# Group norm's inverse deviations on Pool, the rotation tables' memory given back earlier, and two sets of small products placed later

## The chip, the cores and the metric

One core of a Trainium2 chip runs the whole layer in one launch. The metric is device time in microseconds (us). Engines by their names in the profile: PE does the matmuls and PEld loads their weights, DVE is the vector engine, ACT the scalar engine, POOL (Pool in the text) the GpSimd engine, SP issues DMAs.

## The reference

One inference step of a hybrid decoder layer on 256 prompt positions and 8 sequences of 8 new positions, 320 columns in all. It is fp32 throughout. Cut to what matters here:

```
h = rms_norm(x, norm_mix);  u, q, k, v, g = split(h @ w_in)
# S5 group: 64 channel groups, diagonal complex state, scan over positions
xs = associative_scan(a, bu);  y = Re(C xs) + d*u;  y = gelu(y);  s5 = y * sigmoid(y @ w_glu + b_glu)
# retention group: 8 heads of 128, rotary q and k, decay mask
o = ((q k^T) * mask) v + (q r) * q_decay;   r_new = r * decay + (k * k_decay)^T v
mu, var = mean(o), mean((o - mu)^2)                       # group norm over the 128 of a head
o = (o - mu) * rsqrt(var + eps) * ret_gn_w;  ret = silu(g) * o
x = x + concat(s5, ret) @ w_out
x = x + (silu(h2 @ w_gate) * (h2 @ w_up)) @ w_ffn_out,  h2 = rms_norm(x, norm_ffn)
y = rms_norm(x, norm_final)
```

## The kernel before

All activations lie transposed: features on the 128 partitions, the 320 columns in the free dimension. Every large matmul takes a weight block of 128x128 as the stationary operand and 320 columns as the moving one. Each weight is split into a rounded part `hi` (ACT, L128) and a rest `lo` (DVE, L129), the activations likewise, and three matmuls (L139, L140, L141) make one k-step. Blocks of eight k-steps of weights are loaded by SP into three rotating buffers.

The first part of the program (to about 400 us) is the input projection. Between its k-steps stand the small products of eight retention heads and of eight S5 chunks. Where they stand is set by a planner that runs when the program is built: each head and each chunk is a generator, which issues some instructions and then yields a delay; a clock that counts issued matmuls decides after which k-step it goes on. The delays are in the table `DL`. PE and Pool execute their instructions in exactly the order in which the program issues them. DVE and ACT get an order from a scheduler that knows priorities and a model of durations. Every engine works its queue off in order: an instruction that waits holds all behind it.

Names for the steps below. A head `h`: `head_k` transposes the rotated keys `k_` into `pst` and makes the scores `pss`; DVE masks them into `sm` and `smp`. `head_v` transposes the values (`pst2`, which ACT scales into `vT`), makes the outputs `po` and the state product `psr`. Then comes the group norm: DVE's `bn_stats` and `bn_aggr` give mean and variance `mv`, a chain of small instructions on 128x4 makes `gy` (inverse deviation and shift), ACT makes the normalised `on` from `po` and `gy` (L694), and PE transposes it into `pn` (L105), from where it goes to `retp`.

A chunk `c`: DVE makes `bl` and `cl` from the parameters, PE transposes `bl` into `pt`, makes `pk_` (the short kernel) and `pb` (the inputs), DVE rotates by the tables `tab`, scans and rotates back into `xp`, and PE makes the outputs `py`.

`s5_params` makes the parameters on DVE, in scratch space that lies in the two `cl` buffers. Its last products are `lx0`. It then lets Pool clear both `cl` buffers (L448), which has to wait until DVE has read the scratch space for the last time. Pool also makes the rotation tables (`s5_tables`), in four groups of eight pairs.

After the projection: `fin` makes the final states with the last column of `tab`; `split_r` splits the heads' results into `r4a` (heads 0 to 3, in the buffer of the tag "tab") and `r4b`; then `w_out` with `r4a` first, the GLU, `w_out` with its output, and the FFN from about 533 us to the end. `ffn_norm` makes the norm of the FFN's input between the first k-steps of the FFN.

Of the kernel before, what the change touches and what calls it, by code (L numbers as in the profile page):

```python
# [12 lines left out]
F32 = mybir.dt.float32  # L13
# [3 lines left out]
ALU = mybir.AluOpType  # L17
ADD, SUB, MUL = ALU.add, ALU.subtract, ALU.mult
PSUM = bass.MemoryType.PSUM

P = 128
# [9 lines left out]
EPS = 1e-6  # L31
LPAST = 2048
CH = 4
NCP = NP // CH
NC = N // CH
TAIL = ((0, 1), (1, 2), (2, 3), (3, 5), (5, 8), (8, 11))
NPAIR = 32
# [7 lines left out]
def hybrid_kernel(ctx, tc, xT, w_in, w_out, w_glu, w_fi, w_fo, vecs, s5p, bc, x0,  # L45
# [3 lines left out]
    pe, act, dve, pool, sp = nc.tensor, nc.scalar, nc.vector, nc.gpsimd, nc.sync  # L49

    cst = ctx.enter_context(tc.tile_pool(name="cst", bufs=1))
# [8 lines left out]
    make_identity(nc, ident)  # L60
    ones = cst.tile([P, P], F32, name="ones")
    pool.memset(ones, 1.0)
    vec = cst.tile([P, vecs.shape[1]], F32, name="vec")
    bmk = cst.tile([P, 4], F32, name="bmk")

# [2 lines left out]
    o = 0  # L68
# [97 lines left out]
    def ts(out, a, s1, o1, s2=None, o2=None):  # L166
        if o2 is None:
            dve.tensor_scalar(out, a, s1, None, o1)
        else:
            dve.tensor_scalar(out, a, s1, s2, o1, o2)  # L170
        return out
# [5 lines left out]
    def stt(out, a, s, b, o1, o2):  # L177
        dve.scalar_tensor_tensor(out, a, s, b, o1, o2)
        return out

    def rsqrt(t, y, tmp):

        ts(y.bitcast(I32), t.bitcast(I32), -0.5, MUL, float(0x1EF759DF), ADD)
        for _ in range(3):
            tt(tmp, y, y, MUL)
            tt(tmp, tmp, t, MUL)
            stt(y, tmp, 1.5, y, ADD, MUL)
# [104 lines left out]
    prm = s5.tile([P, 3, NPAIR], F32, name="prm")  # L292
    x0t = s5.tile([P, 2, NPAIR, NB], F32, name="x0t")
    tab = s5.tile([P, 2, NPAIR, NCP], F32, name="tab", tag="tab", bufs=1)
    rr = s5.tile([P, NPAIR], F32, name="rr")
    r4 = s5.tile([P, NPAIR], F32, name="r4")
    ff = s5.tile([P, 2, NPAIR], F32, name="ff")
# [159 lines left out]
    def s5_tables(ec, es, g):  # L457
        js = slice(8 * g, 8 * g + 8)
        pool.memset(tab[:, 0, js, 0:1], 1.0)
        pool.memset(tab[:, 1, js, 0:1], 0.0)  # L460
        m, lev = 1, 2
        while m < NCP:
            shm = [P, 8, m]
            er = ec[:, lev, js].unsqueeze(2)
            ei = es[:, lev, js].unsqueeze(2)
            c0, s0 = tab[:, 0, js, 0:m], tab[:, 1, js, 0:m]
            c1, s1 = tab[:, 0, js, m:2 * m], tab[:, 1, js, m:2 * m]
            if m == 1:
                pool.tensor_copy(c1, er)
                pool.tensor_copy(s1, ei)  # L470
            else:
                er, ei = er.to_broadcast(shm), ei.to_broadcast(shm)
                ta = s5.tile([P, 8, 32], F32, name="ta", tag="ta", bufs=1)[:, :, :m]
                pool.tensor_tensor(c1, c0, er, MUL)
                pool.tensor_tensor(ta, s0, ei, MUL)
                pool.tensor_tensor(c1, c1, ta, SUB)
                pool.tensor_tensor(ta, s0, er, MUL)
                pool.tensor_tensor(s1, c0, ei, MUL)
                pool.tensor_tensor(s1, s1, ta, ADD)
            m *= 2  # L480
            lev += 1
            yield 2.0 if g else 0.0


# [10 lines left out]
    def s5_chunk(c):  # L495
# [21 lines left out]
        for w_, pc in ((0, gpc), (1, lpc)):  # L517
# [14 lines left out]
            for g in range(2):  # L532
                ps_, hs = slice(64 * g, 64 * g + 64), slice(16 * g, 16 * g + 16)
                if w_:
                    tt(cl[ps_, 0, :, 1:, hs], m1[ps_, 0:4], m2[ps_, 4:8], SUB)
                    tt(cl[ps_, 1, :, 1:, hs], m1[ps_, 4:8], m2[ps_, 0:4], SUB)
        yield DL["b1"]
        bst = s5.tile([P, 8, P], F32, name="bst", tag="bst", bufs=1)[:, 0:4]
        pt = misc("pt")
        for i in range(4):  # L540
# [94 lines left out]
        return a  # L635

    def head_k(h, q_, qg, k_, R):
        yield DL["k"]
        pst = misc("pst")
        for i, s in enumerate(STARTS):  # L640
            tr(pst[:, P * i:P * i + P], k_[:, s:s + P])
        kd = mp.tile([P, 2, P], F32, name="kd", tag="kd", bufs=1)
        for i in range(2):
            act.mul(kd[:, i], pst[:, P * i:P * i + P], kdc[:, h, i:i + 1])
        act.mul(kv[64:128, h], pst[64:128, 2 * P:3 * P], kdc[64:128, h, 2:3])
        pss = misc("pss")
        mm(0.43, pss[:, 0:256], k_[:, 0:P], q_[:, 0:256], start=True, stop=True)
        mm(0.22, pss[:, 256:384], k_[:, P:256], q_[:, P:256], start=True, stop=True)
        mm(0.22, pss[:, 384:448], k_[:, 192:320], q_[:, 256:320], start=True, stop=True)
        sm = mp.tile([P, 384], F32, name="sm", tag="sm", bufs=1)  # L650
        mk = R["mk"]
        tt(sm[:, 0:256], pss[:, 0:256], mk[:, 0:NP], MUL)
        tt(sm[:, 256:384], pss[:, 256:384], mk[:, 0:P], MUL)
        tt(smp[64:128, :, 0:NS], pss[64:128, 384:448].rearrange("p (b t) -> p b t", t=NS),
           mk[64:128, NP:320].rearrange("p (b t) -> p b t", t=NS), MUL)
        R["kd"], R["sm"] = kd, sm

    def head_v(h, v_, qg, rt, R):
        yield DL["v"]
        pst2 = misc("pst2")  # L660
        for i, s in enumerate(STARTS):
            tr(pst2[:, P * i:P * i + P], v_[:, s:s + P])
        vT = mp.tile([P, 3, P], F32, name="vT", tag="vT", bufs=1)
        for i in range(3):
            act.mul(vT[:, i], pst2[:, P * i:P * i + P], rtok[:, i:i + 1])
        act.copy(kv[0:64, h], vT[64:128, 2])
        yield DL["o"]
        kd, sm = R["kd"], R["sm"]

        po = ps_v.tile([P, 4, P], F32, name="po", tag="po", bufs=1)  # L670
        mm(0.22, po[:, 0], sm[:, 0:P], vT[:, 0], start=True, stop=True)
        mm(0.22, po[:, 1], sm[:, P:256], vT[:, 0], start=True, stop=False)
        mm(0.22, po[:, 1], sm[:, 256:384], vT[:, 1], start=False, stop=True)

        for g in range(2):
            mm(0.22, po[:, 2 + g], smp[:, 4 * g:4 * g + 4].rearrange("p b t -> p (b t)"), vT[:, 2],
               start=g == 0, stop=False, skip_group_check=True)
        for g in range(2):
            for j in range(4):
                mm(0.06, po[32 * j:32 * j + 32, 2 + g], qg[:, 4 * g + j], rt[:, 4 * g + j], start=False,  # L680
                   stop=True, tile_position=(0, 32 * j), skip_group_check=True)
        st = mp.tile([P, 4, 6], F32, name="st", tag="st", bufs=1)
        mv = mp.tile([P, 2, 4], F32, name="mv", tag="mv", bufs=1)
        y = mp.tile([P, 2, 4], F32, name="gy", tag="gy", bufs=1)
        with tc.high_priority(offset=GN):
            for i in range(4):
                dve.bn_stats(st[:, i], po[:, i])
                dve.bn_aggr(mv[:, :, i], st[:, i])
            ts(mv[:, 1], mv[:, 1], -0.5, MUL, -0.5 * EPS, ADD)
            rsqrt(mv[:, 1], y[:, 0], y[:, 1])  # L690
            stt(y[:, 1], mv[:, 0], -1.0, y[:, 0], MUL, MUL)
        on = mp.tile([P, 4, P], F32, name="on", tag="on", bufs=1)
        for i in range(4):
            act.activation(on[:, i], po[:, i], AF.Identity, scale=y[:, 0, i:i + 1],  # L694
                           bias=y[:, 1, i:i + 1])
        psr = misc("psr")
        mm(0.22, psr[:, :P], kd[:, 0], vT[:, 0], start=True, stop=False)
        mm(0.22, psr[:, :P], kd[:, 1], vT[:, 1], start=False, stop=True)
        rp = mp.tile([P, P], F32, name="rp", tag="rp", bufs=1)
        act.copy(rp, psr[:, :P])  # L700
        sp.dma_start(rp_o[h], rp)
        yield DL["c"]
        pn = misc("pn")
        for i in range(4):
            tr(pn[:, P * i:P * i + P], on[:, i])
        pairs_ = ((pn[:, 0:NP], retp[:, h, 0:NP], slice(0, NP)),
                  (pn[:, NP:].rearrange("p (b t) -> p b t", t=32)[:, :, 0:NS],
                   retp[:, h, NP:].rearrange("p (b t) -> p b t", t=NS), slice(NP, N)))
        sg = R.get("sgt")
        for i_, o, sl in pairs_:  # L710
            if sg is None:
                act.mul(o, i_, v("gn", h))
            else:
                g_ = sg[:, sl]
                if sl.start:
                    g_ = g_.rearrange("p (b t) -> p b t", t=NS)
                stt(o, i_, v("gn", h), g_, MUL, MUL)
        R["gn"] = True
        if sg is not None:
            R["sg"] = True  # L720
# [56 lines left out]
    def do_g(h):  # L777
        ps = proj(11 + 4 * h)
        sg = mp.tile([P, N], F32, name="sg", tag="sg", bufs=2)
        with tc.high_priority(offset=EVAC):  # L780
# [4 lines left out]
        run_due()  # L785

    DL = dict(b1=14.2, k1=2.2, b2=4.6, scan=15.6, x=2.2, k=5.5, v=6.1,
              o=2.2, u=6.0, c=10.0, n2=1.6, n2b=2.4, nm=7.8)
    T0, PER = 52.6, 34.0


# [115 lines left out]
    def fin(out, src, m, shape):  # L907
# [9 lines left out]
    finp = s5.tile([P, 2, NPAIR], F32, name="finp", tag="m0", bufs=1)  # L917
    fins = s5.tile([P, 2, NPAIR, NB], F32, name="fins", tag="m1", bufs=1)
    fin(finp.unsqueeze(3), [endp[:, r].unsqueeze(2) for r in range(2)],
        [tab[:, r, :, NCP - 1:] for r in range(2)], [P, NPAIR, 1])  # L920
    fin(fins, [ends[:, 0, r] for r in range(2)],
        [lp[:, r, CH - 1].unsqueeze(2).to_broadcast(shx) for r in range(2)], shx)
    tt(fins, fins, ends[:, 1], ADD)
# [297 lines left out]
```

## Time and profile before

| what | value |
|---|---|
| median of 3 runs | 1487.84 us |
| the three runs | 1484.17 to 1488.72 us |
| the profiled execution | 1486.59 us, its span 1484.8 us |
| PE busy | 1453.6 us, 98% of the span |
| DVE, ACT, Pool busy | 58%, 41%, 5% |
| granted clock of PE, mean | 0.993 |

The span runs from the first instruction's start to the last one's end; the profiled execution's own time is 1.8 us longer. PE is busy nearly throughout, so the profile is read by the few places where PE waits, and by the granted clock.

### The profile page before, as it was taken

The numbers are of one execution on the slowest core, as the hardware profiler recorded it, in microseconds if no ns is written. First come the engines' busy times: TensorE is split into PE (matmuls) and PEld (weight loads), VectorE is DVE, ScalarE is ACT, GpSimd is POOL, SyncE is SP. The second block draws the span as 40 slices with busy tenths as digits, with TensorE's granted clock in tenths as the row PEclk, the third lists the DMA queues.
The fourth block names the chain that finished last, engine by engine and source line by source line (L and its number), as shares of the span: only waits on it lengthen the run. The fifth ranks groups of instructions, "written<-read, shape, count | busy, mean of one in ns | idle before, by whom it ended". The sixth has DMA issues, their size and how long they took to land.

```text
span 1484.8 us, 26198 instructions
## 1 busy us (share of the span) xinstructions
PE 1453.6 (98%) x10654; PEld 1430.8 (96%) x10654; DVE 860.6 (58%) x1507; ACT 616.2 (41%) x988; POOL 76.4 (5%) x159
## 2 busy tenths in 40 slices
PE   8999999999899999999999999999999999999997
PEld 7989998988899999999999999999999999999996
DVE  8998777666646765665445444444444444444454
ACT  6555555554435543333333333333333333333352
POOL 1395000000000000000000000000000000000001
PEclk9999999999999999999999999999999999999998
DMA  7444444442544466665444345444445544445443
GB/s 272 156 154 137 151 143 147 132 127 90 193 153 146 148 210 195 214 213 187 155 146 152 121 152 168 157 153 146 139 137 153 172 152 149 150 123 154 149 147 110
DMA packets 82313, 232.10 MB, mean 156 GB/s; under 512 B 17809, under 2 KB 30225, under 8 KB 82193
## 3 DMA queue, kind: packets, MB, share of 16 engines
q1 hardware_dynamic: 82048, 230.39, 48.4%
q8 instruction: 84, 1.38, 0.4%
q14 instruction: 37, 0.30, 0.1%
q10 hardware_dynamic: 144, 0.04, 0.0%
HBM read 219.35 MB, written 8.95 MB: 154 GB/s over the span
## 4 chain that ended last, share of the span: by engine, by line
PE 68%; DVE 1%; ACT 0%; issue 0%; DVEq 0%
PE ps_fo L141 7%; PE ps_fu L141 7%; PE ps_fu L140 7%; PE ps_fo L139 7%; PE ps_fo L140 7%; PE ps_fu L139 7%; PE ps_fg L141 7%; PE ps_fg L140 7%; PE ps_fg L139 7%; PE ps_o L139 1%; PE ps_o L140 1%; PE ps_o L141 1%; PE ps_g L140 1%; PE ps_g L141 1%; PE ps_g L139 1%; DVE x L174 0%
## 5 line engine op out<-in xcount | busy, mean ns | idle before, releaser
L129 DVE TENSOR_TENSOR lo<-raw,hi 128x1024 fp32r<-128x1024 f32 (+1 forms) x420 | 472.7, 1126 | 398.9 <-ACT hi L128 397.5
L128 ACT CAST hi<-raw 128x1024 fp32r<-128x1024 f32 (+1 forms) x420 | 406.7, 969 | 700.9 <-PE ps_fo L140 189.0
L139 PE MATMUL ps_fg<-hhi,hi 128*128 128x320 f32 x704 | 217.6, 309 | 0.0
L140 PE MATMUL ps_fo<-alo,hi 128*128 128x320 f32 x704 | 217.5, 309 | 0.0
L141 PE MATMUL ps_fo<-ahi,lo 128*128 128x320 f32 x704 | 217.5, 309 | 0.0
L139 PE MATMUL ps_fo<-ahi,hi 128*128 128x320 f32 x704 | 217.5, 309 | 0.0
L141 PE MATMUL ps_fg<-hhi,lo 128*128 128x320 f32 x704 | 217.4, 309 | 0.0
L140 PE MATMUL ps_fu<-hlo,hi 128*128 128x320 f32 x704 | 217.4, 309 | 0.0
L139 PE MATMUL ps_fu<-hhi,hi 128*128 128x320 f32 x704 | 217.4, 309 | 0.0
L141 PE MATMUL ps_fu<-hhi,lo 128*128 128x320 f32 x704 | 217.4, 309 | 0.0
L140 PE MATMUL ps_fg<-hlo,hi 128*128 128x320 f32 x704 | 217.3, 309 | 0.0
L139 PE MATMUL ps_p<-xhi,hi 128*128 128x320 f32 x576 | 183.5, 319 | 0.0
L141 PE MATMUL ps_p<-xhi,lo 128*128 128x320 f32 x576 | 178.1, 309 | 0.0
L140 PE MATMUL ps_p<-xlo,hi 128*128 128x320 f32 x576 | 177.9, 309 | 0.0
L140 PEld LDWEIGHTS ps_fg<-hlo,hi 128*128 128x128 f32 x704 | 132.4, 188 | 0.4
L139 PEld LDWEIGHTS ps_fg<-hhi,hi 128*128 128x128 f32 x704 | 132.3, 188 | 0.3
L139 PEld LDWEIGHTS ps_fo<-ahi,hi 128*128 128x128 f32 x704 | 132.4, 188 | 0.0
L140 PEld LDWEIGHTS ps_fu<-hlo,hi 128*128 128x128 f32 x704 | 132.4, 188 | 0.0
L141 PEld LDWEIGHTS ps_fo<-ahi,lo 128*128 128x128 f32 x704 | 132.4, 188 | 0.0
L139 PEld LDWEIGHTS ps_fu<-hhi,hi 128*128 128x128 f32 x704 | 132.4, 188 | 0.0
L141 PEld LDWEIGHTS ps_fu<-hhi,lo 128*128 128x128 f32 x704 | 132.4, 188 | 0.0
L141 PEld LDWEIGHTS ps_fg<-hhi,lo 128*128 128x128 f32 x704 | 132.3, 188 | 0.0
(415 smaller groups left out, 1971.9 us busy)
## 6 DMA issues: line engine op xcount, KB each, us to landing
raw<-w_fi SPq DMA_DIRECT2D x176, 512.0 KB
raw<-w_in SPq DMA_DIRECT2D x76, 512.0 KB
raw<-w_fo SPq DMA_DIRECT2D x64, 512.0 KB
raw<-w_out SPq DMA_DIRECT2D x32, 512.0 KB
raw<-w_fo SPq DMA_DIRECT2D x64, 192.0 KB
rt<-r SPq DMA_DIRECT2D x8, 512.0 KB
raw<-w_glu SPq DMA_DIRECT2D x8, 512.0 KB
raw<-r SPq DMA_DIRECT2D x8, 512.0 KB
```

The costliest lines, as they stand in the source:

```text
L128: act.copy(hi[:, :m], raw[:, :m])
L129: dve.tensor_tensor(lo[:, :m], raw[:, :m], f(hi[:, :m]), SUB)
L139: pe.matmul(ps, hi, xhi[:, k], start=k == 0, stop=False)
L140: pe.matmul(ps, hi, xlo[:, k], start=False, stop=False)
L141: pe.matmul(ps, lo, xhi[:, k], start=False, stop=k == nk - 1)
```

## The change

Four things.

The chain of the group norm moves from DVE to Pool. Before, DVE made the inverse square root by an integer estimate and three Newton steps, with a shift: twelve instructions on 128x4 for each head. Now Pool does it in eight: the negative mean, the variance plus epsilon, a power of -0.5, one Newton step, and the shift. `bn_stats` and `bn_aggr` stay on DVE.

The last column of the tables is copied into a small tile `tabl` by Pool, once for each group, and `fin` reads that; so the buffer of `tab` is free when the last chunk has rotated back.

The first chunk's `pt` and the first head's `pst` are placed later: their delays grow by 4.0 and 2.5 units of the planner's clock. All that follows in this chunk and this head moves along.

The FFN's norm is placed later: `n2` grows from 1.6 to 3.0.

```
+    mhalf = cst.tile([P, 4], F32, name="mhalf")
+    pool.memset(mhalf, -0.5)
...
+    tabl = s5.tile([P, 2, NPAIR], F32, name="tabl")
...                                                   # s5_tables
+            if m == NCP:
+                pool.tensor_copy(tabl[:, :, js], tab[:, :, js, NCP - 1])
...                                                   # s5_chunk
-        yield DL["b1"]
+        yield DL["b1"] + (4.0 if c == 0 else 0.0)
...                                                   # head_k
-        yield DL["k"]
+        yield DL["k"] + (2.5 if h == 0 else 0.0)
...                                                   # head_v
-            ts(mv[:, 1], mv[:, 1], -0.5, MUL, -0.5 * EPS, ADD)
-            rsqrt(mv[:, 1], y[:, 0], y[:, 1])
-            stt(y[:, 1], mv[:, 0], -1.0, y[:, 0], MUL, MUL)
+
+        m_, t_, y_, w_ = mv[:, 0], mv[:, 1], y[:, 0], y[:, 1]
+        pool.tensor_scalar(m_, m_, -1.0, None, MUL)
+        pool.tensor_scalar(t_, t_, EPS, None, ADD)
+        pool.tensor_tensor(y_, t_, mhalf, ALU.pow)
+        pool.tensor_tensor(w_, y_, y_, MUL)
+        pool.tensor_tensor(w_, w_, t_, MUL)
+        pool.tensor_scalar(w_, w_, -0.5, 1.5, MUL, ADD)
+        pool.tensor_tensor(y_, y_, w_, MUL)
+        pool.tensor_tensor(w_, m_, y_, MUL)
...
-              o=2.2, u=6.0, c=10.0, n2=1.6, n2b=2.4, nm=7.8)
+              o=2.2, u=6.0, c=10.0, n2=3.0, n2b=2.4, nm=7.8)
...                                                   # fin
-        [tab[:, r, :, NCP - 1:] for r in range(2)], [P, NPAIR, 1])
+        [tabl[:, r].unsqueeze(2) for r in range(2)], [P, NPAIR, 1])
```

What the change does to the order of instructions is shown at three places. Line numbers of the changed kernel are higher, and buffer numbers differ.

Pool's queue at the end of the first group of tables. `cl` are the two scratch buffers that are cleared; `mv` and `gy` belong to head 0. Before:

```order
L478 TENSOR_TENSOR tab<-tab,ecs 128x8x32
L479 TENSOR_TENSOR tab<-tab,ta 128x8x32
L448 MEMSET cl_133 128x1280
L448 MEMSET cl_134 128x1280
L459 MEMSET tab 128x8
L460 MEMSET tab 128x8
L469 COPY tab<-ecs 128x8
```

Pool's queue at the same place, now:

```order
L486 COPY tabl<-tab 128x2x8
L451 MEMSET cl_136 128x1280
L451 MEMSET cl_137 128x1280
L696 TENSOR_SCALAR mv<-mv 128x4
L697 TENSOR_SCALAR mv<-mv 128x4
L698 TENSOR_TENSOR gy<-mv,mhalf 128x4
L699 TENSOR_TENSOR gy<-gy 128x4
L700 TENSOR_TENSOR gy<-gy,mv 128x4
L701 TENSOR_SCALAR gy<-gy 128x4
L702 TENSOR_TENSOR gy<-gy 128x4
L703 TENSOR_TENSOR gy<-mv,gy 128x4
L462 MEMSET tab 128x8
```

Head 0's chain stands behind the two clears. The chains of the other heads stand between the later groups of tables, which before followed one another at once.

PE's queue at head 0, where the projection's `ps_p` is interrupted. Before, the keys (`pst` from `k__770`) and the scores come first, then the values (`pst_847`), then six k-steps, then `po`:

```order
L105 MATMUL pst<-ident,k__770 128x128 x3
L100 MATMUL pss<-q__762,k__770 128x256
L100 MATMUL pss<-q__762,k__770 128x128
L100 MATMUL pss<-q__762,k__770 128x64
L105 MATMUL pst_847<-ident,v__774 128x128 x3
L139 MATMUL ps_p<-xhi,hi 128x320
L140 MATMUL ps_p<-xlo,hi 128x320
L141 MATMUL ps_p<-xhi,lo 128x320
```

PE's queue at head 0 now; the values have been transposed four k-steps earlier, two k-steps later than the keys stood before:

```order
L107 MATMUL pst<-ident,k__774 128x128 x3
L102 MATMUL pss<-q__766,k__774 128x256
L102 MATMUL pss<-q__766,k__774 128x128
L102 MATMUL pss<-q__766,k__774 128x64
L102 MATMUL po<-vT,sm 128x128 x3
L102 MATMUL po<-vT,smp 128x128 x2
L102 MATMUL po<-rt,qg_110 32x128 x8
L102 MATMUL psr<-vT,kd 128x128 x2
```

`po` follows `pss` with no k-step between. From `psr` on the distance to `pn` is the same in both, 26 k-steps; `pt` of chunk 0 stands 20 k-steps behind `pn` instead of 10.

DVE's queue at the end of the projection, where `r4a` is split. Before, it stands behind the reads of `tab` by `fin`:

```order
L174 TENSOR_TENSOR cl_134<-endp,tab 128x32 x2
L174 TENSOR_TENSOR fins<-cl_134 128x256
L174 TENSOR_TENSOR y_4975<-y_4975,y_4974 128x320
L174 TENSOR_TENSOR r4a<-retp,r4a 128x320 x4
L178 SCALAR_TENSOR_TENSOR u_114<-y_4975,y_4974 128x320
```

DVE's queue there now:

```order
L176 TENSOR_TENSOR v_4746<-w,tab 128x512
L176 TENSOR_TENSOR v_4747<-w,tab 128x512
L176 TENSOR_TENSOR sg<-ps_p,rbc 128x320
L176 TENSOR_TENSOR xp_135<-v_4746,v_4747 128x4x63 x2
L131 TENSOR_TENSOR lo<-raw,hi 128x1024
L176 TENSOR_TENSOR r4a<-retp,r4a 128x320 x2
L176 TENSOR_TENSOR retp<-retp,sg 128x320
L176 TENSOR_TENSOR r4a<-retp,r4a 128x320 x2
```

`r4a` follows the last chunk's rotation by `tab`, ahead of `fin`.

## The prediction

> **What bounds the kernel now.** I read the page, then PE's waits, then the granted clock by windows, then the timelines of the engines at each wait. The page's first lines:
>
> ```profile
> span 1484.8 us, 26198 instructions
> PE 1453.6 (98%) x10654; PEld 1430.8 (96%) x10654; DVE 860.6 (58%) x1507; ACT 616.2 (41%) x988; POOL 76.4 (5%) x159
> ```
>
> PE is the bound; the change neither adds nor removes a matmul. Only PE's 31.2 us of idle time and its clock can move. PE's waits (total, times, longest), those that the change can touch:
>
> ```profile
> PE pn L105 <- ACT on L694: 4.6, 3, 1.9
> PE ps_o L157 <- ACT r4a L939: 3.8, 1, 3.8
> PE pk__1151 L100 <- DVE qg L174: 2.4, 1, 2.4
> PE pst L105 <- DVE cl L174: 1.4, 1, 1.4
> PE ps_r L100 <- DVE acc L174: 1.0, 1, 1.0
> PE pss L100 <- ACT retp L712: 0.7, 1, 0.7
> PE po L100 <- ACT vT L665: 0.6, 1, 0.6
> PE pst L105 <- ACT kv L645: 0.3, 1, 0.3
> ```
>
> They sum to 14.8 us. The clock adds to that. In these windows the columns after the length are PE, PEld, DVE, ACT, Pool busy, then the clock:
>
> ```profile
> 48.00:115.00 67.00, 62.33 (x543) 59.53 (x542) 63.56 (x177) 37.61 (x89) 51.02 (x101) 1.00 0.48 151
> 339.65:346.47 6.82, 6.08 (x20) 4.98 (x21) 3.99 (x10) 2.15 (x7) 0.00 (x0) 0.50 0.14 57
> 346.47:387.43 40.96, 38.70 (x426) 36.99 (x425) 26.52 (x61) 20.10 (x43) 0.00 (x0) 1.00 0.39 125
> 387.43:394.26 6.83, 5.28 (x18) 4.95 (x19) 5.58 (x17) 2.78 (x7) 0.00 (x0) 0.50 0.92 357
> 394.26:401.09 6.83, 6.83 (x48) 6.83 (x48) 3.34 (x4) 2.10 (x2) 0.00 (x0) 1.00 0.19 62
> ...
> 115.00:339.00 224.00, 219.29 (x2053) 208.68 (x2053) 160.81 (x368) 123.15 (x277) 16.52 (x36) 1.00 0.44 139
> ```
>
> Twice the clock falls to half for 6.83 us: after the last wait for `on`, and within the wait for `r4a`. At half clock the busy time counts twice: 6.08/2 = 3.0 us and 5.28/2 = 2.6 us are lost. At full clock 48 matmuls, 16 k-steps, take 6.83 us: 0.43 us a k-step. From 48 to 115 us DVE is busy 95%: there PE waits for DVE, and the order of queues matters.
>
> **The change part by part.**
>
> *Group norm, heads 4 to 6.* Head 4 (DVE, DVE, PE):
>
> ```profile
> 246.75 0.18 DVE L688 BATCH_NORM_AGGREGATE mv<-st 128x2 f32<-128x6 f32 x1
> 257.90 0.16 DVE L178 SCALAR_TENSOR_TENSOR gy<-mv,gy 128x4 f32<-128x4 f32 x1
> 258.61 1.38 PE L105 MATMUL pn<-ident,on 128*128 128x128 f32 x4 [1.94 <-ACT on L694]
> 72.10 0.45 ACT L694 ACTIVATE on<-po,gy 128x128 f32<-128x128 f32 x1
> ```
>
> The chain's twelve instructions take 0.16 us each but stretch over 11 us, because the scheduler put chunk work between them. PE was ready for `pn` at 256.67; less 0.45 us for the first `on` (last row), Pool may take until 256.2, which is 9.3 us after the variances. Pool's prices:
>
> ```profile
> 52.82 1.23 POOL L469 COPY tab<-ecs 128x8 f32<-128x8 f32 x1 [47.59 <-DVE ecs L174]
> 66.94 0.74 POOL L479 TENSOR_TENSOR tab<-tab,ta 128x256 f32<-128x256 f32 x1
> 75.38 2.27 POOL L448 MEMSET cl<- 128x1280 f32 x2 [7.70 <-DVE lx L174]
> 77.98 0.67 POOL L474 TENSOR_TENSOR tab<-tab,ecs 128x16 f32<-128x16 f32 x1
> 80.62 1.22 POOL L474 TENSOR_TENSOR tab<-tab,ecs 128x32 f32<-128x32 f32 x1
> 111.77 1.67 POOL L475 TENSOR_TENSOR ta<-tab,ecs 128x256 f32<-128x256 f32 x1
> 116.64 0.21 POOL L474 TENSOR_TENSOR tab<-tab,ecs 128x16 f32<-128x16 f32 x1
> 118.08 0.24 POOL L474 TENSOR_TENSOR tab<-tab,ecs 128x32 f32<-128x32 f32 x1
> ```
>
> Six small instructions took from 77.98 to 80.62 (0.44 us each) while DVE was full, and from 116.64 to 118.08 (0.24 each) in calm. Eight make 1.9 to 3.5 us; I take 2.7. The power is not in the trace: its bounds are the cheapest small instruction, 0.21, and the dearest of this engine, 1.67 us. I add 0.4 us, since 128x4 is nearer to the small ones. With 3.1 us against 9.3 the three waits go: -4.6 us. With `pn` on time, the wait of `pss` behind it shrinks too: it waits for `retp` to free a bank, and ACT's queue now has `retp` ahead of `bl`: -0.6. The cause of the first clock drop goes with them: -3.0. Heads 1 to 3 and 7 had no wait for `on` and get none from a chain of 3.1 us. Between the chains now stand table groups, about 19 us each (two of them lie between the same instruction at 77.98 and at 116.64); a head's four projections take 64 k-steps, 27 us, so a group ends before the next chain.
>
> *Group norm, head 0.* Its chain stands behind the two clears of `cl`, and those wait for DVE's `lx` (7.70 us of waiting in the row at 75.38). In the old kernel nobody stood behind that wait except tables needed far later. What DVE and PE do there:
>
> ```profile
> 54.91 0.48 DVE L174 TENSOR_TENSOR k__770<-k__770,sw 128x320 f32<-128x320 f32 x1
> 57.98 0.23 DVE L174 TENSOR_TENSOR smp<-pss,mk 64x64 f32<-64x64 f32 x1
> 66.87 0.16 DVE L170 TENSOR_SCALAR mv<-mv 128x4 f32<-128x4 f32 x1
> 71.51 0.16 DVE L178 SCALAR_TENSOR_TENSOR gy<-mv,gy 128x4 f32<-128x4 f32 x1
> 74.89 0.43 DVE L174 TENSOR_TENSOR lx<-cl 128x256 f32<-128x256 f32 x1
> 55.54 0.52 PE L105 MATMUL pst<-ident,k__770 128*128 128x128 f32 x3 [1.44 <-DVE cl L174]
> 73.94 0.61 PE L105 MATMUL pn<-ident,on 128*128 128x128 f32 x4
> ```
>
> `lx` ended at 75.32. The twelve instructions that leave DVE (66.87 to 71.51, interleaved) free some 0.1 us each, 1.2 us, so `lx` ends at about 74 (73.4 to 74.5, an estimate from these rows). The clears take 2.27: 76.3. Then eight small instructions and the power, at the crowded price: 1.9 to 5, I take 2.5; ACT's first `on` 0.45. So `pn` can start at about 79.2. PE gets there earlier: 73.94, less the 1.7 us of waits that it no longer has before, plus 1.0 us of a new one (next part), is 73.2. **PE waits about 6.0 us for head 0's `on`** (4.5 to 8). A wait of this length will often be followed by half clock. A drop's price is up to 3.4 us, less if its 6.83 us lie partly in the wait; I take 2.0 (0 to 3.4).
>
> On the clock, the Trainium skill, "TensorE: Matmul & The Clock Gate", section "What's actually happening", says that the clock is halved after about 3.4 us without work. The trace agrees only in part: its first drop followed a wait of 1.13 us, while 2.4 us before `pk_` caused none. By that rule the drop after the new wait is certain, and taking it whole the sum below would be 1477.3 us.
>
> *Head 0's keys later.* The waits of 1.44 and 0.27 us go: `k_` was ready at 55.39, and `pst` comes 2.5 us of work later. But `po` now follows `pss` at once, and needs DVE's masks. DVE took from 55.39 to 58.21 to get through `smp`, and now has one `lo` (1.2 us) and `sg` (0.5) ahead of them, so `smp` ends at about 59.9; PE is through with `pss` at about 58.6 (ready at 54.1, six k-steps 2.6, the values 0.5, keys and scores 1.4). Some of `po` overlaps with the later masks: a new wait of 1.0 us (0.3 to 2). Net -0.7.
>
> *Chunk 0 later.* `pt`, `pk_` and `pb` move behind ten more k-steps (4.3 us), and `pk_` waited 2.4 us for `cl`, which DVE now also makes ahead of `retp` and the queries. -2.4. What is late next: `po` of head 1 needs `vT`, 19 k-steps behind `pb`, 8 us or more; DVE and ACT need some 5 of them for the scan. The wait of 0.6 us at that `po` I leave as it is.
>
> *Tables' memory.* The rows of the last chunk:
>
> ```profile
> 374.60 1.29 DVE L174 TENSOR_TENSOR v<-w,tab 128x512 f32<-128x512 f32 x2
> 388.05 0.33 DVE L174 TENSOR_TENSOR cl<-endp,tab 128x32 f32<-128x32 f32 x2
> 388.46 1.54 ACT L939 CAST r4a<-retp 128x320 fp32r<-128x320 f32 x4
> 385.49 1.29 DVE L174 TENSOR_TENSOR r4b<-retp,r4b 128x320 fp32r<-128x320 f32 x3
> 388.98 0.64 PE L157 MATMUL ps_o<-r4a,hi 128*128 128x320 f32 x1 [3.81 <-ACT r4a L939]
> ```
>
> ACT started `r4a` 0.1 us after the last read of `tab`. Without `fin`, that last read is at 375.9: `r4a` is there by about 380, and PE wants it at 385.2. `r4b` is needed eight k-steps, 3.4 us, after that, and was split at 386.8: in time. So -3.8, and the second drop goes: -2.6. The four copies into `tabl` are covered by Pool's idle time.
>
> *FFN norm later.* Placing it three k-steps (1.3 us) later covers the wait of 1.0 us: -1.0. Its result is wanted only when the first FFN product is complete, after 16 k-steps.
>
> The sum: -4.6 -0.6 -3.0 -0.7 -2.4 -3.8 -2.6 -1.0 = -18.7, and +6.0 +2.0 for head 0: -10.7 us. The profiled execution took 1486.6 us, within the 1484.2 to 1488.7 of the runs shown and 1.2 below their median. Forecast **1475.9 us**. About 0.3% (4.5 us) is what a measurement of this kernel can tell from no change.
>
> **The rivals.**
>
> *Head 0 isn't held up.* If the chain's wait is hidden (DVE reaches `lx` about 5 us earlier), the +8.0 is gone: 1467.9 us. For it: DVE's order changes much around there. Against: all the parameter work still precedes `lx`, on a DVE that is 95% busy. Chance 0.10.
>
> *Clock drops come back elsewhere.* If the drops do not follow from these waits, or new short waits cause as many, the 5.6 us are not gained and the one at head 0 costs 3.4: 1475.9 + 5.6 + 1.4 = 1482.9 us. For it: a wait of 1.13 us was enough once. Against: between 115 and 339 us, with the two longer waits for `on`, the clock stayed at 1.00. Chance 0.15.
>
> *The power is dear (slower).* Its price x stands in the chain of every head. Head 0 then waits 5.6 + x with a whole drop of 3.4; heads 4 to 6 have 9.3 us for 2.7 + x. At x = 7.5 the new cost is 16.5 plus 3 x 0.9 against gains of 18.7, so it decides from about 7.5 us on. At 10 us: gains without heads 4 to 6, 10.5; head 0 15.6 + 3.4; heads 4 to 6 wait 3.4 each instead of 1.5, with three drops of 3.0 instead of one, 11.6 more: 1486.6 - 10.5 + 19.0 + 11.6 = 1506.7 us. For it: no row has this operation, and Pool's first instruction after its wait took 1.23 us where later ones took 0.2. Against: 1.67 us is the longest for 64 times as many elements. Chance 0.08. On a first use, the Trainium skill, "GPSIMD Engine Reference", section "Instruction dispatch", gives about 6 us for the first call of a freshly loaded library function; no run here shows one, and head 0 alone would pay it: 1481.9 us.
>
> *Nothing measurable*, by several of these together: 0.05.
>
> **How the numbers follow.** My forecast has 0.62; its own range is 1472 to 1481 from the bounds of the wait (4.5 to 8), the drop (0 to 3.4) and `po` (0.3 to 2). For 8 in 10 it reaches up over most of the returning drops and a little below: 1470 to 1483.5. Faster by over 0.3% means below 1483.4: nearly all of the forecast (0.60), the first rival (0.10) and half of the second (0.08) make 0.78; within 0.3% 0.14; slower 0.08.
>
> **What would show it.** In the new profile: no wait of `pn` for heads 4 to 6, none of `ps_o`, `pk_` and `ps_r`; one wait of about 6 us of `pn` near 73 us, with Pool's clears just before its chain; a wait near 1 us at the first `po`; half clock at most once before 1473 us. I am wrong if `pn` of head 0 does not wait, if the power takes several microseconds, or if half clock shows up where PE hardly waits.

## The result and the profile after

The changed kernel takes 1486.59 us (median of 12 runs), the kernel before 1487.95 us in the same series. The ratio, taken over all the runs and not from the two medians, is 0.9997, 95% interval 0.9987 to 1.0007. That is no change that this measurement can tell. The forecast was 1475.9 us.

The profiled execution took 1487.18 us; that of the kernel before took 1486.59. The top of its page:

```profile
span 1485.4 us, 26187 instructions
...
PE 1450.8 (98%) x10654; PEld 1430.6 (96%) x10654; DVE 849.8 (57%) x1411; ACT 616.5 (42%) x988; POOL 104.1 (7%) x228
```

PE's waits in the changed kernel (total, times, longest); rows of the program's start, and 0.3 us for `ps_g` that both kernels have, are left out:

```profile
PE pn L107 <- ACT on L706: 7.9, 1, 7.9
PE pst L107 <- DVE k__3493 L176: 4.1, 1, 4.1
...
PE pst L107 <- DVE k__3974 L176: 1.9, 1, 1.9
PE ps_r L102 <- DVE ry L180: 1.5, 1, 1.5
PE po L102 <- DVE sm L176: 1.2, 1, 1.2
PE pst L107 <- DVE k__4354 L176: 1.2, 1, 1.2
...
PE pst L107 <- DVE k__2360 L176: 0.7, 1, 0.7
```

All the waits that the change was to remove are gone: `pn` of heads 4 to 6 (4.6 us), `ps_o` (3.8), `pk_` (2.4), `pst` (1.4 and 0.3), `ps_r` for `acc` (1.0), `pss` (0.7). In their place stand the foreseen wait of head 0 (7.9), the foreseen one of `po` (1.2), and new waits for the rotated keys `k_` of heads 5, 6 and 7 (4.1, 1.9, 1.2). PE's idle time grew from 31.2 to 34.6 us.

The clock, by windows (length, busy PE, PEld, DVE, ACT, Pool, then clock, DMA share, GB/s), at the only places of half clock after the start and before the end:

```profile
77.30:87.54 10.24, 5.40 (x20) 4.90 (x21) 5.29 (x12) 5.08 (x14) 9.06 (x30) 0.50 0.22 66
275.27:282.10 6.83, 5.07 (x19) 4.88 (x20) 3.79 (x8) 2.04 (x4) 3.52 (x6) 0.50 0.30 100
```

Both drops of before are gone, and two others are there: about the wait of head 0, and from within the wait for head 5's keys. Half of the busy time is lost: 2.7 + 2.5 us, against 3.0 + 2.6 before.

**Head 0.** Pool's timeline in the changed kernel, from the clears to the last of the chain, and PE's row:

```profile
75.25 2.27 POOL L451 MEMSET cl<- 128x1280 f32 x2 [6.44 <-DVE lx L176]
...
78.62 1.33 POOL L698 TENSOR_TENSOR gy<-mv,mhalf 128x4 f32<-128x4 f32 x1
...
81.39 0.20 POOL L703 TENSOR_TENSOR gy<-mv,gy 128x4 f32<-128x4 f32 x1
82.14 0.82 PE L107 MATMUL pn<-ident,on 128*128 128x128 f32 x2 [7.93 <-ACT on L706]
```

This is the foreseen picture: 6.44 us of standing still, the clears, then the chain. `lx` ended at 75.2 and not at 74, and the chain took 4.1 us, not 2.5.

**Head 4 and head 5's keys.** Timelines of Pool, ACT, DVE and PE in the changed kernel:

```profile
255.35 0.24 POOL L696 TENSOR_SCALAR mv<-mv 128x4 f32<-128x4 f32 x1 [44.14 <-DVE mv L693]
...
256.10 1.92 POOL L698 TENSOR_TENSOR gy<-mv,mhalf 128x4 f32<-128x4 f32 x1
258.10 1.01 POOL L699 TENSOR_TENSOR gy<-gy 128x4 f32<-128x4 f32 x1
...
260.57 0.65 POOL L703 TENSOR_TENSOR gy<-mv,gy 128x4 f32<-128x4 f32 x1
...
261.25 1.51 ACT L706 ACTIVATE on<-po,gy 128x128 f32<-128x128 f32 x4 [3.70 <-POOL gy L703]
...
263.14 1.07 ACT L130 CAST hi<-raw 128x1024 fp32r<-128x1024 f32 x1
264.24 0.42 ACT L634 COPY sw<-ps_p 64x320 f32<-64x320 f32 x1
...
264.25 1.22 DVE L131 TENSOR_TENSOR lo<-raw,hi 128x1024 fp32r<-128x1024 f32 x1 [3.08 <-ACT hi L130]
...
269.81 1.58 DVE L176 TENSOR_TENSOR m<-raw_bc,lpc 128x512 f32<-128x512 f32 x2
271.43 2.25 DVE L176 TENSOR_TENSOR cl<-m,m 64x256 f32<-64x256 f32 x4
...
276.09 0.89 DVE L176 TENSOR_TENSOR k__3493<-k__3493,sw 128x320 f32<-128x320 f32 x1
277.03 0.90 PE L107 MATMUL pst<-ident,k__3493 128*128 128x128 f32 x3 [4.14 <-DVE k__3493 L176]
```

Read from top to bottom it is one chain. Pool's eight instructions take 6.0 us from the last variance at 255.2 to 261.2. ACT has `on` at the head of its queue and waits 3.70 us for it; a weight's `hi` and the queries' `sw` stand behind. DVE needs that `hi` for `lo` and stands still for 3.08 us, with the queries, the chunk's work and the keys behind it. PE is ready for the keys at 272.9 and gets them at 277.03. In the kernel before, ACT had `on` behind the queries' `sw`, which did not have to wait for it:

```profile
252.36 0.43 ACT L629 COPY sw<-ps_p 64x320 f32<-64x320 f32 x1
...
258.10 1.50 ACT L694 ACTIVATE on<-po,gy 128x128 f32<-128x128 f32 x4 [2.25 <-DVE gy L178]
```

### The profile page after: what moved, and what is told of

It is laid out like the page before. It is cut to its first block, busy times and chain, and to the rows that moved or that the text cites. A ratio compares the mean times of both kernels' runs of the same rounds, so it can differ in the third digit from the quotient of the medians.

```text
span 1485.4 us, 26187 instructions
## 1 busy us (share of the span) xinstructions
PE 1450.8 (98%) x10654; PEld 1430.6 (96%) x10654; DVE 849.8 (57%) x1411; ACT 616.5 (42%) x988; POOL 104.1 (7%) x228
## 3 DMA queue, kind: packets, MB, share of 16 engines
q8 instruction: 84, 1.38, 0.4%
## 4 chain that ended last, share of the span: by engine, by line
PE 68%; DVE 1%; DMA 0%; ACT 0%; issue 0%; DVEq 0%; SPq 0%
PE ps_fo L142 7%; PE ps_fu L143 7%; PE ps_fo L143 7%; PE ps_fu L141 7%; PE ps_fu L142 7%; PE ps_fo L141 7%; PE ps_fg L143 7%; PE ps_fg L141 7%; PE ps_fg L142 7%; PE ps_o L141 1%; PE ps_o L142 1%; PE ps_o L143 1%; PE ps_g L142 1%; PE ps_g L143 1%; PE ps_g L141 1%; DMA raw<-w_fi 0%
## 5 line engine op out<-in xcount | busy, mean ns | idle before, releaser
L142 PEld LDWEIGHTS ps_fo<-alo,hi 128*128 128x128 f32 x704 | 132.1, 188 | 0.0
```

The costliest lines, as they stand in the source:

```text
L142: pe.matmul(ps, hi, xlo[:, k], start=False, stop=False)
```

## The experiments

Two theories. The *order theory*: head 0's wait comes from the clears ahead of the chain on Pool, and the keys' waits from ACT's queue, where `on` stands ahead of what DVE needs. The rival: Pool's additional work beside DVE makes both slow, whoever waits for whom. The Trainium skill, "GPSIMD Engine Reference", section "Specifications", says that Pool shares its SBUF interfaces with VectorE and that they collide when DVE reads two SBUF inputs. The rows agree: the same multiply on 128x4 takes 1.01 us at 258.10, beside DVE, and 0.20 in head 7's chain, where DVE is idle (rows in the last section).

All ratios are to the kernel before, with 95% intervals. The changed kernel's own ratio is from another series, so a cost worked out as a difference of two ratios is known to 2 or 3 us.

**Head 0's chain back on DVE.**

```
+        if h == 0:
+            with tc.high_priority(offset=GN):
+                ts(mv[:, 1], mv[:, 1], -0.5, MUL, -0.5 * EPS, ADD)
+                rsqrt(mv[:, 1], y[:, 0], y[:, 1])
+                stt(y[:, 1], mv[:, 0], -1.0, y[:, 0], MUL, MUL)
+        else:
             m_, t_, y_, w_ = ...   # Pool's eight, as they were
```

> The changed kernel, but head 0 alone takes its inverse deviations on DVE again. Order theory (Pool's clears, which wait for DVE's lx, stand ahead of head 0's chain): the 7.9 us wait of pn at 82 us goes, and the 10.24 us of half clock that follow it with it, less about 1 us that the twelve instructions put back on DVE: 10 to 12 us off, 1475 to 1477 us. Rival (the wait comes from a DVE that is late by itself there, whoever makes the deviations): pn of head 0 still waits 4 us or more, and the time stays within 3 us of the changed kernel's 1486.6.

1477.09 us, 0.9926 (0.9914 to 0.9939). `pn` of head 0 has no row left in PE's waits, and the half clock there is gone. The wait and its drop cost about 10.6 us together (0.9997 - 0.9926).

**Only the clears moved.** `pool.memset(t_, 0.0)` of the two `cl` becomes `dve.memset`; the chain stays on Pool. The scheduler also puts DVE's and ACT's instructions around them in another order.

> The changed kernel, but the two clears of cl are done by DVE, right behind lx, so that nothing on Pool stands ahead of head 0's chain that waits; the chain itself stays on Pool. Clears theory: the chain follows head 0's variances at 65 us, behind the first table group's last instructions, and is through by about 74; pn of head 0 waits less than 1 us instead of 7.9, no half clock at 77 us, keys' waits of heads 5 to 7 as they were: 1476 to 1479 us (DVE pays some 2 to 3 us for the clears in a stretch where it is nearly full, and part of it may show at chunk 0's products). Rival (Pool's instructions are so slow beside a full DVE that the chain itself makes head 0 late): pn still waits 3 us or more, 1481 us or more.

1480.59 us, 0.9959 (0.9947 to 0.997). Pool's timeline and two of PE's waits in it:

```profile
69.19 0.24 POOL L696 TENSOR_SCALAR mv<-mv 128x4 f32<-128x4 f32 x1
...
69.81 2.00 POOL L698 TENSOR_TENSOR gy<-mv,mhalf 128x4 f32<-128x4 f32 x1
...
73.29 0.26 POOL L703 TENSOR_TENSOR gy<-mv,gy 128x4 f32<-128x4 f32 x1
...
PE ps_p L143 <- DVE lo L131: 0.9, 2, 0.7
PE pk__1201 L102 <- DVE cl L176: 0.8, 1, 0.8
```

The chain follows the tables at once, is through at 73.5, and `pn` does not wait, though the power takes 2.00 us here. So it was the clears. The time is 1.6 us above what I expected: DVE pays for the clears (1.12 us each), and PE, now with small waits for `lo`, `cl` and the like, is idle for 2.6 us between 76 and 94 us.

**ACT's `on` later, heads 4 to 6.** DVE and Pool keep the same instructions in the same order; on PE one `pn` moves by a k-step:

```
-        for i in range(4):
-            act.activation(on[:, i], po[:, i], AF.Identity, ...)
         psr = misc("psr")
...
-        yield DL["c"]
+        yield DL["c"] - 1.5
+        with tc.issue_after(last_ins["sw"].ins):   # last copy of the newest rotation
+            for i in range(4):
+                act.activation(on[:, i], po[:, i], AF.Identity, ...)
+        yield 1.5
```

> The changed kernel, but for heads 4 to 6 ACT takes the four normalisations (on) after the rotation's copies (sw) of the next head's queries instead of ahead of them; nothing else moves but one pn on PE. Order theory (the keys of heads 5 to 7 are late because ACT stands still at on, waiting for Pool's 6 us chain, with a weight cast and sw queued behind): the waits of pst for the keys, 4.1, 1.9 and 1.2 us, fall below 1 us each, no half clock at 275 us: 7 to 10 us off, 1477 to 1480 us. Rival (Pool's instructions beside DVE make DVE slow, ACT's order does not matter): these waits stay within 1 us of what they were, the time within 3 us of 1486.6.

1477.81 us, 0.9931 (0.9919 to 0.9944). PE's waits, and DVE's timeline at the place shown above:

```profile
PE pn L107 <- ACT on L708: 8.4, 1, 8.4
...
260.75 1.22 DVE L131 TENSOR_TENSOR lo<-raw,hi 128x1024 fp32r<-128x1024 f32 x1
...
265.88 1.34 DVE L176 TENSOR_TENSOR m<-raw_bc,lpc 128x512 f32<-128x512 f32 x2
267.25 1.63 DVE L176 TENSOR_TENSOR cl<-m,m 64x256 f32<-64x256 f32 x4
...
271.08 0.49 DVE L176 TENSOR_TENSOR k__3493<-k__3493,sw 128x320 f32<-128x320 f32 x1
```

The keys' waits of heads 5 to 7 are gone, though Pool's chain still takes its 6 us there. `lo` follows without a stop. The order is the cause, and it costs about 9.8 us with its drop. The rival has a part in the size: `m` and `cl`, which now stand elsewhere beside Pool's tables, take 1.34 and 1.63 us instead of 1.58 and 2.25; in the kernel before, with Pool idle there, they took 1.29 and 1.53. The keys end 5.4 us earlier than in the changed kernel. Of that, 3.5 us are the earlier start of `lo`; from this start to the end of the keys DVE takes 10.8 us instead of 12.7, and those 1.9 us are the stretching.

**The power left out.** `ALU.pow` becomes `MUL` in every head.

> The changed kernel with Pool's power replaced by a multiply of the same shape; it leaves the power out, all else stays. The power's row is 1.92 us in heads 4 to 6 and 1.33 in head 0, a multiply 0.2 to 0.5, so the chains are some 1.5 and 1 us shorter. Order theory: the keys' waits shrink by as much, 4.1 to about 2.6, 1.9 to 0.4, 1.2 to nothing, and head 0's pn from 7.9 to 6.9: 5 us off, 1481 to 1482 us, a little less if the half clock at 275 us goes. Rival (DVE slowed by Pool): only head 0 changes, 1485.5 us.

1482.78 us, 0.9965 (0.9951 to 0.9979). PE's waits, and the multiply of head 4 in Pool's timeline:

```profile
PE pn L107 <- ACT on L706: 7.5, 1, 7.5
PE pst L107 <- DVE k__3493 L176: 3.2, 1, 3.2
...
PE pst L107 <- DVE k__3974 L176: 1.1, 1, 1.1
...
PE pst L107 <- DVE k__4354 L176: 0.3, 1, 0.3
...
254.96 1.08 POOL L698 TENSOR_TENSOR gy<-mv,mhalf 128x4 f32<-128x4 f32 x1
```

Each of the keys' waits is 0.8 to 0.9 us shorter, where I expected 1.5; head 0's is 0.4 shorter, where I expected 1.0, and the time is 0.8 us above the expected range. The chain of head 4 became shorter by 0.7 only (6.0 to 5.3): beside this DVE the multiply takes 1.08 us in the power's place. Nor was the power 1.92 us in all three heads: in head 6 of the changed kernel it took 1.04. The waits follow the chain; the power itself is the smaller part of it.

**Pool's chain beside, unused.**

> The changed kernel, but DVE's old chain feeds on in every head; Pool does its eight instructions all the same, on tiles of its own that nobody reads (power of 1 instead of the variance). So Pool is as busy as in the changed kernel, its instructions stand in the same places, and nobody waits for them. Order theory: no wait of 7.9 us in head 0, no keys' waits over 1 us, the waits of pn in heads 4 to 6 back (4.6 us in all), one half clock: about 1477 us. Rival (DVE slowed by Pool): the keys' waits of heads 5 to 7 are there, 2 us or more for head 5, with DVE's instructions as stretched as in the changed kernel: 1482 us or more.

1479.38 us, 0.9941 (0.9929 to 0.9954). PE's waits:

```profile
PE pn L107 <- ACT on L712: 4.8, 3, 2.1
...
PE pst L107 <- DVE k__2402 L176: 0.6, 1, 0.6
```

The old waits for `on` are back (4.8 us), none is left for the keys of heads 5 to 7, with Pool 107.0 us busy. Pool's work as a neighbour alone makes no keys late. The time is 2 us above the expected 1477; two pieces of half clock of 3.41 us follow the waits for `on`. The kernel is 8.8 us faster than before although Pool's chain runs unused: moving the norm's result to Pool took back nearly all that the other parts had gained.

**Each part alone on the kernel before.** The tables' last column; the two delays; the group norm on Pool.

> The kernel before with the last columns of the tables copied out and read by the final states, nothing else of the change. The prediction's terms: the wait for r4a 3.8 us and the half clock in it 2.6: 6.4 us off, about 1482 us. Rival (the half clock comes back elsewhere, or something else holds r4a): the wait of ps_o goes or stays, the time is within 4 us of before's 1488.

1480.9 us, 0.9955 (0.9942 to 0.9968): -6.7 us, as expected, but not by quite the expected way. Both drops of before are absent, the first of them too, which this edit was not to touch; two shorter ones stand after two other waits for `on`, so 3.4 us are lost instead of 5.6. Half clock is not tied to one place:

```profile
259.82:263.23 3.41, 3.41 (x15) 3.41 (x15) 1.11 (x4) 1.43 (x3) 0.00 (x0) 0.50 0.07 26
300.78:304.19 3.41, 3.41 (x13) 3.24 (x14) 1.91 (x5) 1.81 (x6) 0.00 (x0) 0.50 0.35 130
```

> The kernel before with only the two delays, of chunk 0's first products (4.0) and of head 0's keys (2.5). The prediction's terms: pk_ -2.4, pst -1.7, po +1.0 to 1.2, pss -0.6 or 0: 3 to 3.7 us off, 1484.5 to 1485.5 us. Rival (DVE is the bound in that stretch, so what PE no longer waits for there it waits for later): pk_ and pst go, other waits before 115 us take their place, 1487 to 1488 us.

1484.55 us, 0.998 (0.9968 to 0.9992): -3.0 us, as expected.

> The kernel before with only the group norm on Pool. Order theory: gone the pn waits of heads 4 to 6 (4.6 us) and the half clock after them (3.0); come head 0's wait of 7 to 9 us with up to 5 us of half clock, and keys' waits of 6 to 7 us in heads 5 to 7 with a half clock of 2 to 3; r4a's wait and its half clock stay: 9 to 13 us slower, 1497 to 1501 us. Rival (head 0's wait exists only because chunk 0 was moved): pn of head 0 waits under 4 us, 1490 us or less.

1492.93 us, 1.0036 (1.0023 to 1.0049), +5.4 us. PE's waits:

```profile
PE pn L107 <- ACT on L703: 7.7, 1, 7.7
PE pst L107 <- DVE k__3488 L176: 4.1, 1, 4.1
PE ps_o L159 <- ACT r4a L948: 3.8, 1, 3.8
```

The waits are the expected ones, so head 0's wait does not come from the delays. The time is 4 us below the lower end of my estimate: I had not taken off the wait for `pk_` (2.4 us), which head 0's wait covers, and the half clock was shorter. For the first reason the parts do not add: the 2.4 us are gained by the delays alone and by the norm alone, but only once together. Alone the parts make -6.7 - 3.0 + 5.4 = -4.3 us, together -0.4.

**Both remedies.** Head 0 on DVE, `on` later in heads 4 to 6, and `n2=2.6, n2b=3.0`.

> The two remedies together in the changed kernel: head 0's deviations on DVE, and ACT's on of heads 4 to 6 behind the rotation's copies; besides, the FFN norm's two steps at 2.6 and 3.0 us instead of 3.0 and 2.4. Order theory: the two gains add (9.5 and 8.8 us) and the FFN norm's wait of 1.5 us gets below 1: 1467 to 1469 us, with no wait of pn or of the keys above 1 us and no half clock between 50 and 1460 us. Rival (the waits are one slack that is only handed on, so that the next late engine takes back most of the second gain): 1472 us or more.

1469.59 us, 0.9882 (0.9867 to 0.9898): faster than both kernels, and 0.6 us above the expected range. The longest of PE's waits:

```profile
PE psu L1085 <- issue: 2.7, 1, 2.7
```

No half clock between 50 and 1460 us. No wait for `on`, nor for the keys of heads 5 to 7, is left. The two gains alone are 10.6 + 9.8 = 20.4 us; together, with the FFN's norm besides, they make 17.1. Most of both gains is kept; the missing 3.3 us may lie in the 2.7 us of `psu` at 575 us, which stand in no other profile here, but what these are stays open.

## Why the prediction was wrong

By its terms (us; measured from the rows above, and from the experiments where one isolates the term):

| term | predicted | measured |
|---|---|---|
| `pn` of heads 4 to 6: the waits | -4.6 | -4.6 |
| the same `pn`: within PE's busy time | none | -2.4 |
| `pss` | -0.6 | -0.7 |
| first half clock | -3.0 | -3.0 |
| head 0's keys (old waits, new `po`) | -0.7 | -0.5 |
| chunk 0, `pk_` | -2.4 | -2.4 |
| `r4a` and its half clock | -6.4 | -6.4 (alone, whole kernel: -6.7) |
| FFN norm | -1.0 | +0.5 |
| head 0's `pn`, then half clock | +6.0, +2.0 | +7.9, +2.7 (undone: -10.6) |
| keys of heads 5 to 7, then half clock | none | +7.2, +2.5 (undone: -9.8) |

Two small waits besides, `po` for `vT` gone (-0.6) and head 3's keys (+0.7), cancel. The measured column sums to +0.8 us; the profiled executions differ by +0.6.

The second row is a term that the prediction did not have. A view of PE's waits shows the wait ahead of the first of four transposes. Each of the other three also had to wait for its own `on`, and that time stands as busy: the four of heads 4 to 6 took 1.38, 1.38 and 1.48 us before and take 0.60 each now, as here in head 4:

```profile
264.78 0.60 PE L107 MATMUL pn<-ident,on 128*128 128x128 f32 x4
```

**The step that failed** is the one on heads 4 to 6. It gave Pool 9.3 us, "until 256.2", because PE was not ready for `pn` earlier, and ended there: "With 3.1 us against 9.3 the three waits go". They did go. But PE was not the only one who waits for `gy`: ACT does, and the step never asked what stands behind `on` on ACT. With ACT's `on` moved back and all else left, the kernel takes 1477.8 us, within the forecast's own range of 1472 to 1481. So this missing term is what takes the time out of the range; the other misses (head 0 +2.6 us, the FFN's norm +1.5, the transposes -2.4) partly cancel, which is luck.

The chain's price is the other half of it: 3.1 us was estimated, 6.0 measured in heads 4 and 5 and 5.8 in head 6. The power was put at 0.4 with bounds of 0.21 and 1.67; it took 1.92 in heads 4 and 5, 2.00 in head 0 where only the clears were moved. The small ones were priced at their mean among the tables' instructions, 0.24 to 0.44, and took up to 1.22. Without the wrong order the size would have been harmless: 6.0 is still less than 9.3, and with `on` moved back no `pn` of these heads waits. Without the wrong size the order would have cost little: the waits for the keys shrank about as much as the chain when the power was left out, so a chain 2.9 us shorter would leave about 1.2 of the 7.2 us. That is an estimate; no run has so short a chain.

**Head 0** was right in its mechanism, at the upper end of its size (4.5 to 8 predicted, 7.9 measured). The step that failed there is `lx`: the twelve instructions that left DVE were to end it 1.2 us earlier, but it ended 0.1 us earlier. The chain, 4.1 us instead of 2.5, is the rest. The drop was longer than I allowed (10.24 us, part of it within the wait).

**The FFN norm** failed in its second half: three k-steps later PE no longer waits for the sums (`acc`), but two `lo` of 1.23 us came between DVE's Newton steps, where one had stood before, and PE waited 1.5 us for the result. With the two delays split otherwise, that wait was gone too.

**The rivals.** Half clock did come back elsewhere, as the second rival had it, and about as much as had gone (5.2 against 5.6 us); it came with the two long new waits, and each drop went with its wait. Which wait a drop follows is partly chance, though: with the tables' last column alone all three waits for `on` were still there, and the first drop of before was absent. So its 3.0 us belong to the waits for `on` together, not to the last of them. The dear power did not decide: at 1.0 to 2.0 us it lies far below the 7.5 us at which it would have. Head 0 was held up.

## What to carry to other kernels

When a producer moves to another engine, follow its result to every engine that takes it, and read what stands behind the taker in its in-order queue: here the final consumer had 9 us of slack, and ACT, in between, had too little for a chain of 6 us. Before giving work to an engine's queue, look for an instruction ahead of it that waits for somebody else; two clears that waited for DVE cost about 10.6 us, and moving them alone returned 5.7. Durations of tiny instructions on Pool are those of the place where they run, so take them from rows beside an equally busy DVE. And where several small matmuls each wait for their own operand, look at their durations too, since only the first wait shows as one.

## What the runs showed of the hardware

Beside a busy DVE Pool's instructions on 128x4 stretch: in head 4 the power about twofold, a multiply fivefold. The windows of head 4's and head 7's chains in the changed kernel (length, busy PE, PEld, DVE, ACT, Pool), and head 7's power and first multiply, against 1.92 and 1.01 us in head 4:

```profile
255.30:261.20 5.90, 5.90 (x42) 5.90 (x41) 5.73 (x10) 1.71 (x6) 5.30 (x9) 1.00 0.55 154
368.10:371.20 3.10, 3.10 (x23) 3.10 (x22) 0.00 (x0) 0.71 (x3) 2.50 (x8) 1.00 0.46 151
...
368.75 1.04 POOL L698 TENSOR_TENSOR gy<-mv,mhalf 128x4 f32<-128x4 f32 x1
369.87 0.20 POOL L699 TENSOR_TENSOR gy<-gy 128x4 f32<-128x4 f32 x1
```

Which of them stretches depends on what DVE does at that moment. In head 6 the power took 1.04 us, as in calm, and the first multiply 1.22: it began 0.06 us behind a `lo` on DVE and ended 0.05 us behind it.

```profile
340.62 1.23 DVE L131 TENSOR_TENSOR lo<-raw,hi 128x1024 fp32r<-128x1024 f32 x1
340.68 1.22 POOL L699 TENSOR_TENSOR gy<-gy 128x4 f32<-128x4 f32 x1
```

Half clock came in pieces of 3.41 us: 3.41, 6.83 and 10.24 in these windows. The Trainium skill, "TensorE: Matmul & The Clock Gate", section "What's actually happening", describes a free-running window of 3413 ns; the lengths agree. Its section "Why this matters for your kernels" asks for no gap above about 3 us; here drops followed some waits of 1.1 to 2.1 us of PE for `on` (each with further small gaps between the transposes behind it), so shorter waits are not safe. They are not certain to cost a drop either: in the kernel before, the waits of 1.94 and 1.50 us had none and that of 1.13 had one, and the 2.4 us before `pk_` caused none in the two profiles that have them.
